# Two gate rows of a two-block kernel: 32-column ones matmuls and row copies in place of full-width sums

## The chip, the cores and the metric

One core of one Trainium2 chip runs the whole kernel. The time is device microseconds of one execution, the median of several; a profiled execution gives the trace, whose span runs from the first to the last instruction.

## What is computed

Two transformer blocks follow each other over 256 tokens of width 1024, all in float32. The first is modulated by a vector `c`: six rows of 1024 come from one matrix product, and two of them, `gt1` and `gt2`, gate the two branches of the block.

```python
mod = jax.nn.silu(c) @ w_ada[l] + b_ada[l]
sh1, sc1, gt1, sh2, sc2, gt2 = jnp.split(mod[:, None, :], 6, axis=-1)
...
o = jnp.concatenate([o_mla, o_ret.astype(o_mla.dtype)], axis=-1) @ w_out[l]
x_new = x + gt1 * o
x_new = x_new + gt2 * conv_ffn(modulate(rmsnorm(x_new, g_norm2[l]), sh2, sc2),
                               w_up[l], conv_w[l], conv_b[l], w_down[l])
```

The change touches `gt1` and `gt2` alone. The mixer of the block (latent attention, `w_uq` and `w_ukv` among its weights, and retention) and the second block stay as they are.

## The kernel before

The 256 tokens lie on partitions in two tiles of 128. Each float32 product is made of three matmuls of a high and a low part: a weight tile of 128x1024 (512 KB) is loaded by a DMA from SyncE's queue into one of five `raw` buffers (L211, L213), ScalarE casts it to the high part (L223, or L230 with a gain), VectorE takes the difference for the low part (L226, L231), and TensorE uses both (L186). A `raw` buffer comes free when the low part is made, and SyncE's next load waits for that. SyncE issues in program order, so a transfer that waits holds all that stand behind it.

The instructions of each engine are put in order by a scheduler that goes by estimated costs and priorities; a change in one place can move instructions around it.

The modulation rows come in two ways. Rows 0 and 1 are made on TensorE at the start (`ada_unit`). Rows 2 to 5 are made by `tick` (L518 to L534), which is called between other pieces of work: it loads one of eight `w_ada` tiles of a row (L524), and VectorE multiplies it by `silc`, one value for each partition, and adds it to an accumulator `g` of 128x1024 (L527, L530). After the eighth tile `ada_done` (L497) sums the accumulator over its 128 partitions with a matmul against a tile of ones. For rows 3 and 4 (shift and scale of the second branch) this is done in four matmuls of 32 columns of ones (L509), each of which puts 256 of the 1024 sums onto 32 partitions of one PSUM tile `tr`. For rows 2 and 5, the gates, two matmuls with 128 columns of ones (L503) put 512 sums each on all 128 partitions, and VectorE adds them (L505) onto `gt1` or `gt2`, tiles `bc` of 128x1024 that hold the bias row on every partition. Two DMAs (L494, L495, issued by L127 in `bc_row`) spread the bias from DRAM at about 64 us.

```python
                for i in range(2):
                    t = tr_tile()
                    ac = slice(i * 512, (i + 1) * 512)
                    nc.tensor.matmul(t, lhsT=ones, rhs=acc[:, ac], start=True, stop=True)
                    d = dst[:, i * 512:(i + 1) * 512]
                    nc.vector.tensor_tensor(out=d, in0=d, in1=t, op=ALU.add)
```

Around gate 1 (110 us) the program is in the input projection and the latent attention's `w_uq`. The `w_uq` product for the first 128 tokens goes into the two `at` tiles of PSUM, ScalarE reads them (L676), VectorE rotates 32 columns of each head (L631, L635, and the sum L637), and TensorE transposes the result (L682); then the same for the second 128 tokens in the same `at` tiles. The keys follow from `w_ukv` (L695). Two DMAs copy rotated keys inside SBUF, from 32 partitions to 32 others, four times each (L658). Around gate 2 (232 us) it is in the retention's heads (L772 to L807), and the `w_out` tiles arrive. `gt1` is read by VectorE behind `w_out`'s matmuls (L920) and `gt2` behind `w_down`'s (L1320).

Of the kernel before, what the change touches and what calls it, by code (L numbers as in the profile page):

```python
# [9 lines left out]
F32 = mybir.dt.float32  # L10
# [4 lines left out]
ALU = mybir.AluOpType  # L15
# [3 lines left out]
P = 128  # L19
# [39 lines left out]
ROW_COLS = {}  # L59
_o = 0  # L60
for _n, _w in (("g_ret", 512), ("onorm", 128), ("sinks", 8), ("ret_decay", 8), ("g_final", 1024),
               ("g_mix_post", 1024), ("g_x_post", 1024), ("g_ffn_post", 1024), ("g_mix_pre", 1024), ("b_gt1", 1024), ("b_gt2", 1024)):
    ROW_COLS[_n] = (_o, _o + _w)
    _o += _w
NROW = _o
# [17 lines left out]
def body(tc, A, out):  # L83
    nc = tc.nc
    es = ExitStack()
    with es:
        _body(nc, tc, A, out, es)


def _body(nc, tc, A, out, es):  # L90
# [18 lines left out]
    def tr_tile():  # L109
        return ps.tile([P, 512], F32, tag="tr", name="tr", bufs=2)  # L110
# [12 lines left out]
    def bc_row(dst, name, a=0, b=None):  # L123
        o, e = ROW_COLS[name]
        e = e if b is None else o + b
        o = o + a
        nc.sync.dma_start(dst, A["rows"][0:1, o:e].broadcast_to([P, e - o]))  # L127
# [3 lines left out]
    ones = cp.tile([P, P], F32, name="ones")  # L131
# [157 lines left out]
    with ExitStack() as e1:  # L289
        p1 = lambda name, bufs=1: e1.enter_context(tc.tile_pool(name=name, bufs=bufs))  # L290
        s8 = p1("s8p")
        s = p1("s1")
# [4 lines left out]
        c1 = s.tile([P, NC1 - 128], F32, name="c1")  # L297
# [40 lines left out]
        def ada_fm(acc, bias, dst, ns=1):  # L338
            rows = ada_rows(acc)
            t = tr_tile()  # L340
            for b in range(2):
                nc.tensor.transpose(t[:, b * P:(b + 1) * P], rows[:, b * P:(b + 1) * P], ident)
            tv = t[:, 0:256].rearrange("p (b q n) -> p n q b", b=2, q=4)
            for i in range(ns):
                nc.vector.tensor_tensor(out=dst[:, 8 * i:8 * i + 8].rearrange("p (q b) -> p q b", b=2), in0=tv[:, i, :, :],
                                        in1=FM(bias).rearrange("p (q b) -> p q b", b=2), op=ALU.add)

        def scale_gain(dst, sc, gname):
            nc.vector.scalar_tensor_tensor(out=dst, in0=sc, scalar=1.0, in1=FM(gname), op0=ALU.add, op1=ALU.mult)
# [141 lines left out]

        gt1 = bct()
        gt2 = bct()
        bc_row(gt1, "b_gt1")  # L494
        bc_row(gt2, "b_gt2")  # L495

        def ada_done(g, acc):  # L497
            if g in (2, 5):
                dst = gt1 if g == 2 else gt2
                for i in range(2):  # L500
                    t = tr_tile()
                    ac = slice(i * 512, (i + 1) * 512)
                    nc.tensor.matmul(t, lhsT=ones, rhs=acc[:, ac], start=True, stop=True)  # L503
                    d = dst[:, i * 512:(i + 1) * 512]
                    nc.vector.tensor_tensor(out=d, in0=d, in1=t, op=ALU.add)  # L505
            else:
                t = tr_tile()
                for q in range(4):
                    nc.tensor.matmul(t[32 * q:32 * q + 32, 0:256], lhsT=ones[:, 0:32],  # L509
                                     rhs=acc[:, q * 256:(q + 1) * 256], start=True, stop=True)  # L510
                ada_fm(t, "b_sh2" if g == 3 else "b_sc2", B2 if g == 3 else A2)
            if g == 4:
                scale_gain(A2, A2, "g_norm2")
# [357 lines left out]
    c2 = s2.tile([P, NCST2], F32, name="c2")  # L871
# [532 lines left out]
    for g in range(1, 6):  # L1404
        nb = 4 if g < 5 else 2
        sg = G4()
        for part, mk, us in ((0, tr_tile, ones_w2["gate"][g]), (1, at_tile, ones_w2["up"][g])):
# [3 lines left out]
            for i in range(nb // 2):  # L1411
                c = slice(i * 512, (i + 1) * 512)
                if part == 0:
                    nc.vector.tensor_tensor(out=sg[:, c].rearrange("p (j n) -> p j n", j=2),
                                            in0=accs[i].rearrange("p (j n) -> p j n", j=2),
                                            in1=rbc.unsqueeze(1).broadcast_to([P, 2, T]), op=ALU.mult)
# [17 lines left out]
def _constants():  # L1434
    f = np.float32
    pos = np.arange(T)

    def ang(p, dim):
        inv = (f(10000.0) ** (-np.arange(0, dim, 2, dtype=f) / f(dim))).astype(f)
        return (p.astype(f)[:, None] * inv[None, :]).astype(f)  # L1440

    ar, ac = ang(pos // 64, 16), ang(pos % 64, 16)
    mcos = np.concatenate([np.cos(ar), np.cos(ar), np.cos(ac), np.cos(ac)], 1)
    msin = np.concatenate([-np.sin(ar), np.sin(ar), -np.sin(ac), np.sin(ac)], 1)
    aq = ang(pos, 128)
    rcos, rsin = np.cos(aq), np.concatenate([-np.sin(aq), np.sin(aq)], 1)
    halves = lambda a: np.concatenate([a[:P], a[P:]], 1)
    p = np.arange(P)[:, None]
    j = np.concatenate([np.arange(P)[:, None], P + np.arange(P)[:, None]], 1)
    dl = np.arange(384)[None, :] - 128 - p  # L1450
    i = np.broadcast_to(np.arange(T)[None, :], (P, T))
    c1 = [np.eye(P), halves(mcos), halves(msin), halves(rcos), halves(rsin),
          np.concatenate([255 - j, j], 1), dl + 0 * p, i + 1, T - i]
    c1 = np.concatenate([np.asarray(a, f) for a in c1], 1)
    assert c1.shape == (P, NCST1)
    q = np.arange(P)
    causal = (p // 64 == q[None, :] // 64) & (p <= q[None, :])
    ck = np.arange(T)[None, :] // 64
    cq = 2 + p // 64
    ok = (ck <= cq) & (ck >= cq - 2)  # L1460
    c2 = [causal, np.where(ok, 0.0, -1e30)]
    c2 = np.concatenate([np.asarray(a, f) for a in c2], 1)
    assert c2.shape == (P, NCST2)
    return np.ascontiguousarray(c1), np.ascontiguousarray(c2)


def _layout(I):
    g = lambda n: np.asarray(I[n])
    fmv = lambda a: a.reshape(-1, P).T
    lb = g("hgrn_lb_2")  # L1470
    cw = g("conv_w")[0]
    fm = {"c": g("c"), "c_ctx": g("c_ctx"), "g_norm1": g("g_norm1"), "g_norm2": g("g_norm2"), "g_q": g("g_q"),
          "g_kv": g("g_kv"), "conv0": cw[0], "conv1": cw[1], "conv2": cw[2], "conv_b": g("conv_b"),
          "g_mem": g("g_mem_2"), "g_mix_pre": g("g_mix_pre_2"), "g_x_pre": g("g_x_pre_2"),
          "g_ffn_pre": g("g_ffn_pre_2"), "lb0": lb[0], "lb1": lb[1], "b_sh1": g("b_ada")[0, 0:1024], "b_sc1": g("b_ada")[0, 1024:2048],
          "b_sh2": g("b_ada")[0, 3072:4096], "b_sc2": g("b_ada")[0, 4096:5120]}
    order = np.array([0, 4, 1, 5, 2, 6, 3, 7])
    rows = {"g_ret": g("g_ret"), "onorm": g("hgrn_onorm_2"), "sinks": g("sinks_2"),
            "ret_decay": g("ret_decay"), "g_final": g("g_final"), "g_mix_post": g("g_mix_post_2"),
            "g_x_post": g("g_x_post_2"), "g_ffn_post": g("g_ffn_post_2"), "g_mix_pre": g("g_mix_pre_2"), "b_gt1": g("b_ada")[0, 2048:3072],  # L1480
            "b_gt2": g("b_ada")[0, 5120:6144]}
    w_in2 = g("w_in_2")[0]
    qa = w_in2[:, :512].reshape(D, 8, 64)[:, order].reshape(D, 512)
    w_in2 = np.concatenate([qa, w_in2[:, 512:]], 1)
    w_out2 = g("w_out_2")[0]
    w_out2 = np.concatenate([w_out2[:512].reshape(8, 64, D)[order].reshape(512, D), w_out2[512:]], 0)
    ukv = g("w_ukv")[0].reshape(256, 8, 2, 64).transpose(0, 2, 1, 3).reshape(256, 1024)
    c1, c2 = _constants()
    arrays = {
        "fm": np.concatenate([fmv(fm[n]) for n in FM_COLS], 1),  # L1490
        "rows": np.concatenate([rows[n].reshape(1, -1) for n in ROW_COLS], 1),
        "cst1": c1, "cst2": c2,
        "x": g("x")[0], "ctx": g("ctx")[0], "mem": g("mem_2")[0], "w_ada": g("w_ada")[0], "w_in": g("w_in")[0],
        "w_uq": g("w_uq")[0], "w_ukv": ukv, "w_out": g("w_out")[0], "w_up": g("w_up")[0], "w_down": g("w_down")[0],
        "w_in_2": w_in2, "w_out_2": w_out2, "wq_x": g("wq_x_2")[0], "wk_x": g("wk_x_2")[0], "wv_x": g("wv_x_2")[0],
        "wo_x": g("wo_x_2")[0], "w_gate": g("w_gate_2")[0], "w_up2": g("w_up_2")[0], "w_down2": g("w_down_2")[0],
    }
    return {n: np.ascontiguousarray(a) for n, a in arrays.items()}
# [17 lines left out]
```

## Time and profile before

| | before |
|---|---|
| median of 3 runs | 853.47 us (852.82 to 855.85) |
| profiled execution | 853.53 us |
| its span | 851.7 us |
| TensorE busy | 820.4 us, 96% of the span |
| VectorE busy | 575.3 us, 68% |
| ScalarE busy | 463.2 us, 54% |
| GpSimd busy | 52.7 us, 6% |
| DMA | 154.22 MB, mean 181 GB/s |
| mean granted clock | 0.994 of full speed |

The shares are means over the whole span, and say little on one place. A row of a timeline gives the start, the time in us, the engine and line, the operation and its operands, and in brackets how long the engine had stood idle and for what. SPq is SyncE's queue, where DMAs are issued; the time there is that of the issue, and a DMA's landing is told apart, in the DMA view. PE is TensorE, DVE is VectorE, ACT is ScalarE.

### The profile page before, as it was taken

The numbers are of one execution on the slowest core, as the hardware profiler recorded it, in microseconds if no ns is written. First come the engines' busy times: TensorE is split into PE (matmuls) and PEld (weight loads), VectorE is DVE, ScalarE is ACT, GpSimd is POOL, SyncE is SP. The second block draws the span as 40 slices with busy tenths as digits, with TensorE's granted clock in tenths as the row PEclk, the third lists the DMA queues.
The fourth block names the chain that finished last, engine by engine and source line by source line (L and its number), as shares of the span: only waits on it lengthen the run. The fifth ranks groups of instructions, "written<-read, shape, count | busy, mean of one in ns | idle before, by whom it ended". The sixth has DMA issues, their size and how long they took to land.

```text
span 851.7 us, 12981 instructions
## 1 busy us (share of the span) xinstructions
PE 820.4 (96%) x4978; PEld 691.3 (81%) x4978; DVE 575.3 (68%) x881; ACT 463.2 (54%) x749; POOL 52.7 (6%) x91
## 2 busy tenths in 40 slices
PE   6999988999999999999999999999999999999996
PEld 5767966766687899999997877777788899999995
DVE  4339767996697797667577766775847865656642
ACT  6739262324565675555454757664636844545531
POOL 1100020110110000000002200001001100000000
PEclk9999998999999999999999999999999999999999
DMA  8998786874154566666664553443623676666511
GB/s 289 312 311 274 239 260 206 291 232 134 50 161 141 177 227 197 183 189 182 191 188 149 163 147 121 124 145 114 194 92 120 185 226 191 181 189 188 183 50 50
DMA packets 65150, 154.22 MB, mean 181 GB/s; under 512 B 5184, under 2 KB 10816, under 8 KB 65088
## 3 DMA queue, kind: packets, MB, share of 16 engines
q1 hardware_dynamic: 65088, 153.39, 57.6%
q8 instruction: 39, 0.64, 0.3%
q14 instruction: 23, 0.19, 0.1%
HBM read 151.80 MB, written 1.05 MB: 179 GB/s over the span
## 4 chain that ended last, share of the span: by engine, by line
PE 66%; ACT 3%; DVE 3%; issue 1%; POOL 1%; DVEq 0%; POOLq 0%; ACTq 0%
PE acc L186 32%; PE at L256 12%; PE tr L256 12%; PE tr L168 1%; PE at L1280 1%; PE at L1258 1%; PE tr L1199 1%; DVE xl L226 1%; ACT junk L144 1%; ACT xh L223 1%; PE at L1149 1%; PE at L1151 1%; PE tr L743 0%; PE at L772 0%; PE at L789 0%
## 5 line engine op out<-in xcount | busy, mean ns | idle before, releaser
L223 ACT CAST wh<-raw 128x1024 fp32r<-128x1024 f32 (+1 forms) x90 | 91.0, 1013 | 101.5 <-PE acc L186 27.4
L226 DVE TENSOR_TENSOR wl<-raw,wh 128x1024 fp32r<-128x1024 f32 (+1 forms) x87 | 102.3, 1178 | 46.7 <-ACT wh L223 45.7
L226 DVE TENSOR_TENSOR xl<-raw,xh 128x1024 fp32r<-128x1024 f32 x68 | 84.6, 1248 | 43.0 <-ACT xh L223 42.7
L223 ACT CAST xh<-raw 128x1024 fp32r<-128x1024 f32 x68 | 70.9, 1047 | 55.0 <-PE tr L256 24.6
L186 PE MATMUL acc<-wh,xTh 128*128 128x512 f32 (+2 forms) x272 | 100.0, 394 | 0.3 <-ACT xTh L160 0.3
L186 PE MATMUL acc<-wh,xTl 128*128 128x512 f32 (+2 forms) x272 | 97.3, 382 | 0.0
L186 PE MATMUL acc<-wl,xTh 128*128 128x512 f32 (+2 forms) x272 | 96.7, 380 | 0.5 <-DVE wl L226 0.5
L231 DVE SCALAR_TENSOR_TENSOR wl<-raw,fm,wh 128x512 fp32r<-128x512 f32 (+3 forms) x96 | 67.2, 743 | 42.9 <-ACT wh L230 42.4
L230 ACT ACTIVATE wh<-raw,fm 128x512 fp32r<-128x512 f32 (+3 forms) x96 | 63.7, 712 | 36.5 <-issue 16.5
L186 PEld LDWEIGHTS acc<-wh,xTh 128*128 128x128 f32 x272 | 50.3, 189 | 12.0 <-issue 2.4
L186 PEld LDWEIGHTS acc<-wl,xTh 128*128 128x128 f32 x272 | 50.3, 188 | 11.3 <-issue 2.3
L186 PEld LDWEIGHTS acc<-wh,xTl 128*128 128x128 f32 x272 | 50.4, 188 | 9.6 <-issue 1.0
L186 PE MATMUL acc<-xh,xTl 128*128 128x512 f32 x144 | 53.5, 397 | 0.0
L186 PE MATMUL acc<-xl,xTh 128*128 128x512 f32 x144 | 53.3, 396 | 0.1
L186 PE MATMUL acc<-xh,xTh 128*128 128x512 f32 x144 | 53.2, 397 | 0.0
L231 DVE SCALAR_TENSOR_TENSOR xl<-raw,fm,xh 128x512 fp32r<-128x512 f32 (+1 forms) x44 | 33.3, 797 | 17.8 <-ACT xh L230 17.7
L186 PE MATMUL acc<-xh,g 128*128 128x512 f32 x160 | 44.5, 391 | 0.0
L230 ACT ACTIVATE xh<-raw,fm 128x512 fp32r<-128x512 f32 (+1 forms) x44 | 31.2, 756 | 22.5 <-issue 13.0
L530 DVE SCALAR_TENSOR_TENSOR g<-raw,silc,g 128x1024 f32<-128x1024 f32 x28 | 35.8, 1279 | 6.7 <-DMA raw<-in_w_ada_dram 6.7
L186 PE MATMUL acc<-wh,g 128*128 128x512 f32 x128 | 36.4, 391 | 0.0
L186 PEld LDWEIGHTS acc<-xh,g 128*128 128x128 f32 x160 | 29.7, 188 | 5.8
L186 PEld LDWEIGHTS acc<-xl,xTh 128*128 128x128 f32 x144 | 26.8, 188 | 6.3 <-DVE xl L226 1.1
(375 smaller groups left out, 1751.0 us busy)
## 6 DMA issues: line engine op xcount, KB each, us to landing
raw<-in_w_up_dram SPq DMA_DIRECT2D x66, 512.0 KB, 3.9
raw<-in_w_ada_dram SPq DMA_DIRECT2D x48, 512.0 KB, 5.3
raw<-in_w_down_dram SPq DMA_DIRECT2D x44, 512.0 KB, 3.5
raw<-in_w_in_dram SPq DMA_DIRECT2D x38, 512.0 KB, 3.9
raw<-in_w_gate_dram SPq DMA_DIRECT2D x22, 512.0 KB, 4.0
raw<-in_w_out_dram SPq DMA_DIRECT2D x16, 512.0 KB, 3.6
raw<-in_wk_x_dram SPq DMA_DIRECT2D x8, 512.0 KB, 6.3
raw<-in_wv_x_dram SPq DMA_DIRECT2D x8, 512.0 KB, 5.7
```

The lines of the kernel that those rows point to most:

```text
L144: nc.scalar.activation(junk[:, 0:a.shape[-1]], a, AF.Square, scale=n ** -0.5, accum_out=ss)
L168: nc.tensor.transpose(t[:, j * P:(j + 1) * P], src[:, (b + j) * P:(b + j + 1) * P], ident)
L186: nc.tensor.matmul(accs[i], lhsT=xl if f == 2 else xh, rhs=wl[i] if f == 1 else wh[i], start=first and f == 0, stop=last and f == 2)
L223: nc.scalar.copy(wh[:, 0:n], raw[:, 0:n])
L226: eng.tensor_tensor(out=wl[:, 0:n], in0=raw[:, 0:n], in1=wh[:, 0:n].bitcast(F32), op=ALU.subtract)
L230: nc.scalar.activation(wh[:, s], raw[:, s], AF.Copy, scale=gains[k])
L231: nc.vector.scalar_tensor_tensor(out=wl[:, s], in0=raw[:, s], scalar=gains[k], in1=wh[:, s].bitcast(F32), op0=ALU.mult, op1=ALU.subtract)
L256: nc.tensor.matmul(accs[b // 2][:, (b % 2) * T:(b % 2 + 1) * T], lhsT=wt[:, o:o + P], rhs=xt[:, k, :], start=k == 0 and fl == 0 and b % 2 ...
L530: nc.vector.scalar_tensor_tensor(out=ada_cur[g], in0=raw, scalar=silc[:, k, 0:1], in1=ada_cur[g], op0=ALU.mult, op1=ALU.add)
L1149: nc.tensor.matmul(o[cs, hs], lhsT=ATs[cs, cols], rhs=ih[cs, hs], start=True, stop=cg == 0)
L1151: nc.tensor.matmul(o[cs, hs], lhsT=qi[:, cols], rhs=Sst[cg - 1][:, hs], start=False, stop=True)
L1199: nc.tensor.matmul(sc[:, j * nk:(j + 1) * nk], lhsT=qTs[pr_, hd * P:(hd + 1) * P], rhs=kTs[pr_, 0:nk], start=True, stop=True)
```

## The change

All four rows that `tick` makes are now summed by the four 32-column matmuls. For the gates, VectorE adds the bias to the `tr` tile in one instruction of 128x256 and writes the sum into a tile `bgt`, of which partitions 0, 32, 64 and 96 matter: partition 32q holds quarter q of the row. Then four DMAs from SyncE's queue (L507 in the new numbering) each read one of these partitions, 256 values, and write them to all 128 partitions of a quarter of `gt1` or `gt2`: 1 KB to each of 128 partitions, 128 KB in all. The bias comes with one load of 128x512 (256 KB) from a new array, zero but in those four partitions; the two spread loads of 512 KB each are gone.

```diff
-        bc_row(gt1, "b_gt1")
-        bc_row(gt2, "b_gt2")
+        bgt = s.tile([P, 512], F32, name="bgt")
+        nc.sync.dma_start(bgt, A["bgt"])

         def ada_done(g, acc):
+            t = tr_tile()
+            for q in range(4):
+                nc.tensor.matmul(t[32 * q:32 * q + 32, 0:256], lhsT=ones[:, 0:32],
+                                 rhs=acc[:, q * 256:(q + 1) * 256], start=True, stop=True)
             if g in (2, 5):
                 dst = gt1 if g == 2 else gt2
-                for i in range(2):
-                    t = tr_tile()
-                    ac = slice(i * 512, (i + 1) * 512)
-                    nc.tensor.matmul(t, lhsT=ones, rhs=acc[:, ac], start=True, stop=True)
-                    d = dst[:, i * 512:(i + 1) * 512]
-                    nc.vector.tensor_tensor(out=d, in0=d, in1=t, op=ALU.add)
+                rows = bgt[:, 0:256] if g == 2 else bgt[:, 256:512]
+                nc.vector.tensor_tensor(out=rows, in0=t[:, 0:256], in1=rows, op=ALU.add)
+                for q in range(4):
+                    nc.sync.dma_start(dst[:, q * 256:(q + 1) * 256],
+                                      rows[32 * q:32 * q + 1, :].unsqueeze(1).broadcast_to([1, P, 256]))
             else:
-                t = tr_tile()
-                for q in range(4):
-                    nc.tensor.matmul(t[32 * q:32 * q + 32, 0:256], lhsT=ones[:, 0:32],
-                                     rhs=acc[:, q * 256:(q + 1) * 256], start=True, stop=True)
                 ada_fm(t, "b_sh2" if g == 3 else "b_sc2", B2 if g == 3 else A2)
```

The lines below the change count one less than before. The order of instructions differs between about 70 and 285 us, and is the same after that.

SyncE's queue at gate 1, about 106 to 115 us of the run before (`raw` is a weight buffer, `bc` is `gt1`):

```order
 L213 DMA raw<-in_w_in_dram 128x2x512
-L524 DMA raw<-in_w_ada_dram 128x1024 x3
+L523 DMA raw<-in_w_ada_dram 128x1024 x2
+L507 DMA bc<-bgt 128x1x256 x4
+L523 DMA raw<-in_w_ada_dram 128x1024
 L211 DMA raw<-in_w_ukv_dram 128x1024 x2
+L657 DMA s_1271<-s_1269 32x4x512
```

The four copies stand ahead of one `w_ada` tile and both `w_ukv` tiles, and they wait for VectorE's add.

ScalarE at the same place, where L230 is the cast of the two `w_ukv` tiles and L676 (now L675) the read of the `at` tiles of the first 128 tokens:

```order
+L653 COPY s_1269<-tr 32x512
 L230 ACTIVATE wh<-raw,fm 128x1024
-L160 CAST g_1171<-tr 128x2x128 x2
-L676 ACTIVATE g_1342<-at,rq_1176 128x384
-L654 COPY s_1265<-tr 32x512
-L676 ACTIVATE g_1342<-at,rq_1176 128x384
+L675 ACTIVATE g_1346<-at,rq_1180 128x384 x2
 L230 ACTIVATE wh<-raw,fm 128x1024
```

Both reads stand behind the first cast, before and now; nothing that could go ahead of them is left between.

VectorE some microseconds later, where L530 (now L529) is the accumulate of a `w_ada` tile and L637 (now L636) the sum that ends the rotation of the first 128 tokens:

```order
 L231 SCALAR_TENSOR_TENSOR wl<-raw,fm,wh 128x1024
-L631 TENSOR_TENSOR s1k<-g_1342,c_92 128x256
-L635 TENSOR_TENSOR s1k<-g_1342,c_92 128x16x8 x2
-L530 SCALAR_TENSOR_TENSOR g_1334<-raw,silc,g_1334 128x1024
-L637 TENSOR_TENSOR g_1342<-s1k 128x8x32
+L630 TENSOR_TENSOR s1k<-g_1346,c_92 128x256
+L634 TENSOR_TENSOR s1k<-g_1346,c_92 128x16x8 x2
+L636 TENSOR_TENSOR g_1346<-s1k 128x8x32
 L231 SCALAR_TENSOR_TENSOR wl<-raw,fm,wh 128x1024
```

The accumulate no longer stands ahead of the sum.

SyncE's queue at gate 2, about 230 us of the run before (`bc` is `gt2`):

```order
 L213 DMA raw<-in_w_in_dram 128x2x512 x3
-L211 DMA raw<-in_w_out_dram 128x1024 x8
+L211 DMA raw<-in_w_out_dram 128x1024 x6
+L507 DMA bc<-bgt 128x1x256 x4
+L211 DMA raw<-in_w_out_dram 128x1024 x2
 L213 DMA raw<-in_w_up_dram 128x2x512 x4
```

The four copies stand ahead of the last two `w_out` tiles and of `w_up`.

## Rows read from the trace of the kernel before

**Rows 1.** Busy time by stretch: us of PE, PEld, DVE, ACT, POOL; clock, DMA share, GB/s.

```profile
60.00:70.00 10.00, 8.91 (x48) 5.67 (x48) 6.53 (x17) 7.65 (x13) 0.00 (x0) 1.00 0.85 289
...
126.00:130.00 4.00, 0.00 (x0) 0.00 (x0) 1.67 (x3) 0.95 (x2) 0.00 (x0) 0.87 1.05 187
130.00:134.00 4.00, 3.99 (x14) 3.45 (x15) 3.36 (x6) 1.17 (x2) 0.00 (x0) 0.50 1.01 331
134.00:138.00 4.00, 4.00 (x20) 3.30 (x19) 1.93 (x3) 1.07 (x2) 0.00 (x0) 0.78 0.81 315
...
150.00:160.00 10.00, 10.00 (x56) 7.46 (x55) 9.78 (x17) 3.37 (x7) 0.00 (x0) 1.00 0.88 296
```

**Rows 2.** Chain of waits, gate 2: start us, us, what.

```profile
231.24 1.05 PE tr L503 x2
...
233.19 0.86 PE tr L503 x2
```

**Rows 3.** Timeline of all engines, gate 1, 108 to 115 us.

```profile
110.06 1.88 PE L503 MATMUL tr<-g,ones 128*128 128x512 f32 x4
...
111.36 0.68 DVE L505 TENSOR_TENSOR bc<-bc,tr 128x512 f32<-128x512 f32 x1
111.47 2.53 SPq L211 DMA_DIRECT2D raw<-in_w_ukv_dram  x2
...
113.69 0.50 PE L186 MATMUL acc<-wl,xTh 128*128 128x512 f32 x1 [0.53 <-DVE wl L226]
```

**Rows 4.** DMA view, 110 to 115 us: GB/s in 40 slices, packets, issues with us to landing.

```profile
GB/s 410 344 410 344 311 426 344 262 328 328 328 360 262 360 393 393 328 262 328 328 328 328 328 393 360 393 393 328 492 393 328 426 459 360 360 361 459 328 524 262
DMA packets 510, 1.81 MB, mean 361 GB/s; under 512 B 55, under 2 KB 55, under 8 KB 510
...
raw<-in_w_ukv_dram SPq DMA_DIRECT2D x2, 512.0 KB, 4.8
```

**Rows 5.** PE's waits, 60 to 80 us: total us, times, longest us.

```profile
PE acc L186 <- DVE wl L231: 1.4, 3, 0.5
```

**Rows 6.** Timeline of PE, the 32-column sums of row 3.

```profile
163.26 0.64 PE L509 MATMUL tr<-g,ones 128*32 128x256 f32 x8
```

**Rows 7.** The copies inside SBUF, line 658: issue ns and landing us, min/median/max.

```profile
L658 SPq DMA_DIRECT2D s<-s x2: 755/1080/1405, 122.3 to 123.1; - x2
...
DMA to landing us min/median/max: 8.4/8.7/8.9
```

**Rows 8.** DMA view, 125 to 130 us, while those copies run.

```profile
DMA packets 371, 0.90 MB, mean 180 GB/s; under 512 B 44, under 2 KB 44, under 8 KB 370
...
q1 hardware_dynamic: 370, 0.89, 103.5%
```

**Rows 9.** Timeline of ACT, 118 to 131 us.

```profile
118.32 1.16 ACT L230 ACTIVATE wh<-raw,fm 128x1024 fp32r<-128x1024 f32 x1
...
125.90 1.04 ACT L676 ACTIVATE g<-at,rq 128x384 f32<-128x384 f32 x2
```

**Rows 10.** Timeline of PE, 120 to 137 us: the second w_uq product and what follows.

```profile
123.71 0.51 PE L186 MATMUL at<-wh,s 128*128 128x384 f32 x2
...
130.01 1.94 PE L682 MATMUL tr<-ident,g 128*96 128x128 f32 x8 [4.05 <-DVE g L637]
131.60 1.20 PE L695 MATMUL at<-g,wh 128*128 128x512 f32 x2
```

**Rows 11.** Timeline of DVE, 116 to 132 us: the accumulate ahead of the rotation's sum.

```profile
128.33 1.28 DVE L530 SCALAR_TENSOR_TENSOR g<-raw,silc,g 128x1024 f32<-128x1024 f32 x1 [4.52 <-DMA raw<-in_w_ada_dram]
```

**Rows 12.** Timeline of DVE, gate 2.

```profile
232.50 0.68 DVE L505 TENSOR_TENSOR bc<-bc,tr 128x512 f32<-128x512 f32 x1
```

**Rows 13.** DMA view, 232 to 240 us: issues, KB each, us to landing.

```profile
raw<-in_w_out_dram SPq DMA_DIRECT2D x2, 512.0 KB, 3.6
```

**Rows 14.** Timeline of ACT, gate 2: the cast of the seventh w_out tile.

```profile
239.80 1.05 ACT L223 CAST xh<-raw 128x1024 fp32r<-128x1024 f32 x1 [0.73 <-DMA raw<-in_w_out_dram]
```

**Rows 15.** Timeline of PE, gate 2: a retention head's output matmuls.

```profile
243.08 0.71 PE L801 MATMUL acc<-s1k 128*128 128x128 f32 x4
```

More of the change, by code (lines that the diff above doesn't have):

```diff
@@ L61 @@
 for _n, _w in (("g_ret", 512), ("onorm", 128), ("sinks", 8), ("ret_decay", 8), ("g_final", 1024),
-               ("g_mix_post", 1024), ("g_x_post", 1024), ("g_ffn_post", 1024), ("g_mix_pre", 1024), ("b_gt1", 1024), ("b_gt2", 1024)):
+               ("g_mix_post", 1024), ("g_x_post", 1024), ("g_ffn_post", 1024), ("g_mix_pre", 1024)):
     ROW_COLS[_n] = (_o, _o + _w)
@@ L1479, in _layout @@
             "ret_decay": g("ret_decay"), "g_final": g("g_final"), "g_mix_post": g("g_mix_post_2"),
-            "g_x_post": g("g_x_post_2"), "g_ffn_post": g("g_ffn_post_2"), "g_mix_pre": g("g_mix_pre_2"), "b_gt1": g("b_ada")[0, 2048:3072],
-            "b_gt2": g("b_ada")[0, 5120:6144]}
+            "g_x_post": g("g_x_post_2"), "g_ffn_post": g("g_ffn_post_2"), "g_mix_pre": g("g_mix_pre_2")}
+    bgt = np.zeros((P, 512), np.float32)
+    bgt[::32, 0:256] = g("b_ada")[0, 2048:3072].reshape(4, 256)
+    bgt[::32, 256:512] = g("b_ada")[0, 5120:6144].reshape(4, 256)
     w_in2 = g("w_in_2")[0]
@@ L1491, in _layout @@
         "rows": np.concatenate([rows[n].reshape(1, -1) for n in ROW_COLS], 1),
-        "cst1": c1, "cst2": c2,
+        "cst1": c1, "cst2": c2, "bgt": bgt,
         "x": g("x")[0], "ctx": g("ctx")[0], "mem": g("mem_2")[0], "w_ada": g("w_ada")[0], "w_in": g("w_in")[0],
```

## The prediction

> **What bounds the kernel now.** I read the table of stretches first [rows 1]: TensorE is the engine that is nearly always busy (8.91 us of the ten from 60 us, all of the ten from 150 us), and the one hole near the change is the stretch 126 to 130 us, in which it does nothing. Then the chain of waits at the second gate [rows 2]: both gate matmuls stand on it, 1.05 and 0.86 us. Then the timeline of the first gate [rows 3], for what follows there, and the DMA view of the same time [rows 4]: 110 to 115 us moves 361 GB/s, all sixteen engines at work. So there the transfers are full too, and whatever is put into SyncE's queue there pushes back what stands behind it. 0.5% of this kernel, 4.3 us, is about what a measurement can tell from no change.
>
> **The change, part by part.** The profiled run took 853.53 us, 0.06 above the median of 853.47; I add to 853.53.
>
> *Loads.* Two bias rows of 512 KB each leave, a tile of 256 KB comes, all at 63.7 us. At 361 GB/s that is 768 KB, 2.1 us of transfers. TensorE's waits there are for VectorE's splits, 1.4 us in all between 60 and 80 us [rows 5], none for a load, and I take nothing; the bounds are 0 and -2.1 us.
>
> *Matmuls.* Gate 1: 1.88 us for two full-width matmuls become four 32-column ones, 0.64 us by the group that exists already for g = 3 [rows 6]. The 1.2 us saved is lost at once: at 113.69 us TensorE waits for VectorE's w_in split anyway, 0.53 us, and what starts that split is a load, not the gate. Gate 2: 1.05 + 0.86 = 1.91 us on the chain become 0.64: -1.27 us. VectorE's two adds of 0.68 us per gate [rows 3] become one of half that width, some 0.4 us; VectorE does not set the end at either place.
>
> *The eight copies.* Four per gate, each 128 KB out of one partition into 128. They go into SyncE's queue, each waiting on VectorE's add, ahead of w_ukv at gate 1 and ahead of the seventh w_out tile at gate 2 (the order above). No row shows a copy out of one partition. The nearest are the two s<-s copies at 122 us, 256 KB each out of 32 partitions: their issue takes SyncE 755 and 1405 ns, and they land after 8.4 and 8.9 us [rows 7]. While they run the sixteen engines stay full but move 180 GB/s [rows 8], where loads moved 361: one half. One reading is that a copy runs at the speed of the part of SBUF that it reads from: 32 partitions half of it, one partition a sixteenth. That gives 361/16 = 22.6 GB/s, 5.8 us for 128 KB. As 361 is a mean of loads from DRAM, I also take the best slice of that stretch, 524 GB/s [rows 4], of which a sixteenth is 32.8 GB/s, 4.0 us. From below the bound is a copy as fast as any load: 128 KB at 361 GB/s, 0.36 us. I take the slow reading, because the one copy inside SBUF that the trace has is so slow, and in it the middle of its two rates, 27.7 GB/s: 4.73 us a copy, 18.9 us a gate.
>
> Here the Trainium skill speaks against the change (page "SBUF — State Buffer", section "Door 1: The DMA port swizzle"): four neighbouring partitions lie behind one of sixteen ports, measured at 27.6 GB/s, and partitions 32 apart share a port. By its 27.6 GB/s a copy would be an estimated 4.75 us, and the total 0.2 us above mine; by the row's 22.6 GB/s it would be 8.6 us above. That 180 is half of 361 agrees with its table, in which 32 partitions reach half the ports; that one partition has a sixteenth no row shows.
>
> *Gate 1 on the path.* w_ukv is issued at 111.47 us and lands 4.8 us later [rows 3, 4], at 116.3. With the four copies ahead it lands 18.9 us later, 135.2. ScalarE now has w_ukv's cast ahead of the two reads (L675) that free the `at` tiles, so TensorE's second half of w_uq waits for it: the cast takes 1.16 us, the two reads 1.04 us [rows 9], and TensorE goes on at 137.4 us. Before, its hole ended at 130.01 us, 4.05 us long [rows 10], since the rope sum stood behind an accumulate that waited 4.52 us for its w_ada tile [rows 11]; in the new order that accumulate is behind the rope sum. After the hole the granted clock is 0.50 (the 1.2 GHz level), 0.87 before it and 0.78 after [rows 1]: it fell about 3 us after TensorE had stopped and was at half from about 129.0 to 135.8 us, 5.75 us of it with TensorE at work. I put the same 5.75 us behind the new, longer hole. The work between the hole and the keys' matmuls is now twelve w_uq matmuls, 2.25 us (123.71 to 125.96), and eight transposes, 1.59 us at half clock (130.01 to 131.60), so 0.8 at full: together 3.05 us at full, which at that clock takes 5.93 us: the keys' first matmul, L694 (L695 before), at 143.3. Before, it began at 131.60 with 4.16 us of half clock ahead, worth a start at 133.7 at full clock. Gate 1 costs +9.6 us.
>
> *Gate 2 on the path.* The add ends at about 232.9 us (it began at 232.50) [rows 12]. The transfers are idle there, so the copies start at once and hold the sixteen engines for 18.9 us; the seventh w_out tile, 3.6 us from issue to landing [rows 13], lands at 255.4. Before, its cast began at 239.80, having waited for that landing [rows 14]. That is +15.6 us. ScalarE's cast stands ahead of the copy (L774) and the exponentials (L777) that the next head's output matmuls read, so TensorE stops before those, which began at 243.08 us [rows 15]. A stop this long lowers the clock as the one at 126 us did: from the three stretches 126 to 138 us, 5.75 us at half, +2.9 us. With -1.27 us from the matmuls gate 2 costs +17.2 us.
>
> *No one else waits.* The gates are read behind w_out's and w_down's matmuls (L920, L1320), later than any landing above. If that cover went, it would be the landing itself that is paid.
>
> Sum: 853.53 + 9.6 + 17.2 = 880.3, so 880 us. With 4.0 or 5.8 us a copy the eight give 874.5 or 889.
>
> **The rivals.**
>
> *Copies like s<-s.* The four copies of a gate are 512 KB as those two are, and take 8.7 us together, whatever they read from. For it: it is the row itself, no extrapolation. Against: those 8.7 us hold a wait behind loads already queued. Gate 1: 111.8 + 8.7 + 4.8 = 125.3 for w_ukv, TensorE at 127.5, L694 at 133.4: -0.3 us. Gate 2: 232.9 + 8.7 + 3.6 = 245.2, +5.4 + 2.9 - 1.27 = +7.0. 860 us, 855 to 866.
>
> *Cheap copies, and faster.* If a copy costs no more than its bytes at 361 GB/s, only SyncE's issue is left, four times the median 1.08 us of the s<-s issues, 4.3 us. At gate 1 w_ukv lands at 121.2 us and the reads end at 123.4, before TensorE has done its other work (125.96 less the 2.25 us of w_uq). The hole and the half clock are gone, since the accumulate is out of the way: L694 at 126.8, up to -6.9 us. VectorE, busy 9.78 of the ten us from 150 [rows 1], can't give all of it; I take two thirds, -4.6. Gate 2: +1.0 - 1.27 = -0.3. 848.7 us, 846 to 853. It decides as soon as four copies take less than about 6 us. For it: 361 GB/s out of sixteen engines. Against: no copy inside SBUF in this trace ran near that.
>
> *Nothing but noise.* The order of the program differs from 70 to 285 us for reasons besides the copies, and the stretch could close up around them: within 2 us of before.
>
> **How the numbers follow.** Slow single-partition copies 0.45, copies like s<-s 0.22, cheap ones 0.26, nothing 0.07. Faster than 849.2 us comes from two thirds of the cheap case, 0.17. Within 0.5%: the rest of it 0.09, the nothing 0.07, and 0.02 of the s<-s case: 0.18. Slower: 0.65. The range of 849 to 889 us leaves out 0.16 of the cheap case and 0.04 above the upper price. As cases of both signs hold chances, the likeliest one's own range is 874 to 889.
>
> **What the profile would show.** Right: the copies land 19 us and more after the first one's issue, with transfers full at a rate far under 180 GB/s; TensorE idle some 14 us near 123 to 137 us, ended by ScalarE or VectorE behind the landing of w_ukv, and some 12 us near 243 us behind w_out; clock at 0.5 after each. Wrong: copies landing within 9 us of issue, or TensorE full in both places, or SyncE's own issue times as the longest wait.

## The result, and the profile after

The changed kernel takes 881.88 us (median of 6 runs, 879.02 to 884.28), the kernel before 852.14 (6 runs, 850.66 to 855.85): a ratio of 1.033, 95% interval 1.031 to 1.035, 3.3% slower. The forecast was 880.

The first lines of the page of the changed kernel, the span and the busy time of each engine:

```profile
span 879.5 us, 13009 instructions
...
PE 823.1 (94%) x4986; PEld 692.1 (79%) x4986; DVE 574.8 (65%) x879; ACT 463.4 (53%) x749; POOL 54.1 (6%) x91
```

No engine has much more to do: TensorE is busy 823.1 us against 820.4, VectorE 574.8 against 575.3. The span is 27.8 us longer, so the time went into waits. TensorE's waits between 100 and 300 us in the changed kernel, with the total, the number and the longest, begin with the first two of these lines; the third is a smaller one to which I come back:

```profile
PE at L771 <- ACT s1k L774: 14.4, 1, 14.4
PE at L186 <- ACT g L675: 13.5, 1, 13.5
...
PE tr L168 <- DVE bgt L505: 1.1, 1, 1.1
```

The two are one wait each, and the 4.05 us behind L637 [rows 10] is gone. SyncE's timeline at gate 1, then at gate 2, and the line of the copies (nanoseconds of issue, then us to landing, each minimum, median, maximum):

```profile
113.52 8.84 SPq L507 DMA_DIRECT2D bc<-bgt  x4
122.46 3.59 SPq L523 DMA_DIRECT2D raw<-in_w_ada_dram  x1
126.15 5.10 SPq L211 DMA_DIRECT2D raw<-in_w_ukv_dram  x2
...
244.90 8.28 SPq L507 DMA_DIRECT2D bc<-bgt  x4
253.29 9.06 SPq L211 DMA_DIRECT2D raw<-in_w_out_dram  x2
```

```profile
L507 SPq DMA_DIRECT2D bc<-bgt x8: 557/1406/5190, 113.5 to 248.4; - x8
...
DMA to landing us min/median/max: 7.0/12.7/15.8
```

The copies land after up to 15.8 us, and SyncE itself is held: the four issues of a gate take 8.84 and 8.28 us, one of them 5.19. The DMA view of the changed kernel from 113 to 131 us, GB/s in 40 slices of 0.45 us and the share of the sixteen engines' time:

```profile
GB/s 382 364 209 105 57 34 27 27 20 36 25 27 21 36 25 23 25 36 25 23 25 34 48 84 73 36 23 32 32 23 20 41 73 146 100 41 64 75 93 164
...
q1 hardware_dynamic: 754, 1.22, 78.9%
```

To compare with [rows 4] and [rows 8]: the engines are at work 78.9% of the time and move 20 to 36 GB/s for most of the 12 us from 115 us on. What TensorE waited for at gate 1 and how it went on, ScalarE's timeline and then TensorE's:

```profile
138.07 1.15 ACT L230 ACTIVATE wh<-raw,fm 128x1024 fp32r<-128x1024 f32 x1 [15.20 <-DMA raw<-in_w_ukv_dram]
139.12 1.03 ACT L675 ACTIVATE g<-at,rq 128x384 f32<-128x384 f32 x2
```

```profile
139.74 1.16 PE L186 MATMUL at<-wh,s 128*128 128x384 f32 x2 [13.53 <-ACT g L675]
...
144.82 0.73 PE L694 MATMUL at<-g,wh 128*128 128x512 f32 x2
```

And at gate 2, ScalarE and then TensorE:

```profile
265.55 1.04 ACT L223 CAST xh<-raw 128x1024 fp32r<-128x1024 f32 x1 [16.38 <-DMA raw<-in_w_out_dram]
```

```profile
268.27 2.08 PE L771 MATMUL at<-g,g 128*128 128x128 f32 x8 [14.44 <-ACT s1k L774]
```

Busy time by stretch, columns as in [rows 1]; the clock is the first number behind POOL:

```profile
116.00:120.00 4.00, 3.69 (x13) 2.58 (x12) 2.10 (x10) 2.55 (x9) 2.84 (x7) 0.58 0.82 27
...
128.00:132.00 4.00, 0.00 (x0) 0.00 (x0) 0.00 (x0) 0.00 (x0) 0.00 (x0) 0.70 0.74 131
132.00:136.00 4.00, 0.00 (x0) 0.00 (x0) 1.28 (x1) 0.00 (x0) 0.00 (x0) 0.50 0.95 274
136.00:140.00 4.00, 0.26 (x1) 0.26 (x1) 0.75 (x1) 1.93 (x3) 0.00 (x0) 0.50 1.04 188
140.00:144.00 4.00, 4.00 (x18) 3.61 (x19) 2.97 (x6) 2.23 (x4) 0.00 (x0) 0.60 1.04 299
...
262.00:266.00 4.00, 0.00 (x0) 0.00 (x0) 0.00 (x0) 0.45 (x1) 0.00 (x0) 0.50 0.87 267
266.00:270.00 4.00, 1.73 (x8) 1.73 (x9) 3.15 (x6) 3.53 (x7) 0.00 (x0) 0.50 0.46 151
270.00:274.00 4.00, 4.00 (x23) 3.79 (x22) 1.71 (x4) 2.50 (x5) 0.00 (x0) 0.63 0.61 190
```

**Where the 28 us came from**, by the same instructions in both traces. VectorE's add of gate 1 starts 1.7 us later (113.07 against 111.36). From it to the keys' matmuls at full clock, 31.75 us against 22.34 (111.36 to the 133.7 of the prediction): +9.4. From there to the add of gate 2, 99.6 against 98.8: +0.8. From that add, 244.46 against 232.50, to the first read of `gt1`, 291.87 against 263.87: 47.4 against 31.4, +16.0. Together 28.0, and nothing is given back after that.

### The profile page after: what moved, and what is told of

Read it like the earlier page. It is cut to its first block, busy times and chain, and to the rows that moved or that the text cites. A ratio compares the mean times of both kernels' runs of the same rounds, so it can differ in the third digit from the quotient of the medians.

```text
span 879.5 us, 13009 instructions
## 1 busy us (share of the span) xinstructions
PE 823.1 (94%) x4986; PEld 692.1 (79%) x4986; DVE 574.8 (65%) x879; ACT 463.4 (53%) x749; POOL 54.1 (6%) x91
## 4 chain that ended last, share of the span: by engine, by line
PE 63%; ACT 4%; DVE 3%; DMA 1%; issue 1%; SPq 1%; POOL 1%; DVEq 0%; POOLq 0%; ACTq 0%
PE acc L186 30%; PE at L256 12%; PE tr L256 12%; DMA raw<-in_w_out_dram 1%; PE tr L168 1%; ACT xh L223 1%; SPq L507 1%; PE at L1279 1%; PE at L1257 1%; PE tr L1198 1%; DVE xl L226 1%; ACT junk L144 1%; PE at L1148 1%; PE at L1150 0%; PE tr L742 0%
## 5 line engine op out<-in xcount | busy, mean ns | idle before, releaser
L186 PE MATMUL acc<-wl,xTh 128*128 128x512 f32 (+2 forms) x272 | 99.4, 390 | 0.8 <-DVE wl L226 0.8
L231 DVE SCALAR_TENSOR_TENSOR wl<-raw,fm,wh 128x512 fp32r<-128x512 f32 (+3 forms) x96 | 67.2, 742 | 46.9 <-ACT wh L230 46.3
L230 ACT ACTIVATE wh<-raw,fm 128x512 fp32r<-128x512 f32 (+3 forms) x96 | 63.7, 712 | 51.0 <-issue 16.5
L186 PEld LDWEIGHTS acc<-wh,xTh 128*128 128x128 f32 x272 | 50.4, 189 | 13.5 <-issue 2.3
L529 DVE SCALAR_TENSOR_TENSOR g<-raw,silc,g 128x1024 f32<-128x1024 f32 x28 | 37.8, 1349 | 14.1 <-DMA raw<-in_w_ada_dram 13.9
L231 DVE SCALAR_TENSOR_TENSOR xl<-raw,fm,xh 128x512 fp32r<-128x512 f32 (+1 forms) x44 | 33.3, 797 | 17.8 <-ACT xh L230 17.7
L230 ACT ACTIVATE xh<-raw,fm 128x512 fp32r<-128x512 f32 (+1 forms) x44 | 31.1, 756 | 22.5 <-issue 13.0
```

Of the source, the lines that this page charges most:

```text
L186: nc.tensor.matmul(accs[i], lhsT=xl if f == 2 else xh, rhs=wl[i] if f == 1 else wh[i], start=first and f == 0, stop=last and f == 2)
L230: nc.scalar.activation(wh[:, s], raw[:, s], AF.Copy, scale=gains[k])
L231: nc.vector.scalar_tensor_tensor(out=wl[:, s], in0=raw[:, s], scalar=gains[k], in1=wh[:, s].bitcast(F32), op0=ALU.mult, op1=ALU.subtract)
L529: nc.vector.scalar_tensor_tensor(out=ada_cur[g], in0=raw, scalar=silc[:, k, 0:1], in1=ada_cur[g], op0=ALU.mult, op1=ALU.add)
```

## The experiments

All runs are on one core, beside runs of the kernel before (851.5 to 852.0 us in the median). A run without an interval was executed once; single runs of the kernel before lie up to 6 us from its median, so those are read by their traces.

**What is read, or that it is a copy.** My theory: the price is that of reading one partition. Rivals: a copy inside SBUF is slow by itself, or costs what the s<-s copies did.

```diff
-                                      rows[32 * q:32 * q + 1, :].unsqueeze(1).broadcast_to([1, P, 256]))
+                    nc.sync.dma_start(dst[:, q * 256:(q + 1) * 256], rows)
```

> The four copies of a gate read all 128 partitions of bgt (256 values of each partition go to the same partition of the gate tile) in place of one; bytes, number of copies, their place in SyncE's queue and the order of all engines stay. The gate tiles then hold other values than the sums. If the price comes from reading one partition (my theory): the copies land within 5 us of their issue in place of 7.0 to 15.8, the stretch in which the engines move under 30 GB/s is gone, TensorE's waits of 13.5 and 14.4 us shrink under 2 us, and the time is 846 to 856 us. If a copy inside SBUF is slow whatever it reads from (rival 1): landing and waits as in the changed kernel, 875 to 885 us. If it costs as the s<-s copies did (rival 2): about 8.7 us for four, 857 to 866 us.

849.87 us. The line of the copies in this run:

```profile
L507 SPq DMA_DIRECT2D bc<-bgt x8: 536/598/608, 113.7 to 231.5; - x8
...
DMA to landing us min/median/max: 2.0/2.1/2.1
```

Same bytes, same place in the queue, landed after a sixth of the time (median 2.1 against 12.7 us), and SyncE is not held. No wait of TensorE from 100 to 300 us is over 1.5 us in total. That is the theory's case. It also gives an idea of the time of the change without its price, but no gain is shown: one run of 849.87 us lies within the spread of the kernel before (848.72 to 857.52 beside it).

**Reading 32 partitions**, four times each, which keeps the repeated reading.

```diff
-                    nc.sync.dma_start(dst[:, q * 256:(q + 1) * 256],
-                                      rows[32 * q:32 * q + 1, :].unsqueeze(1).broadcast_to([1, P, 256]))
+                    nc.sync.dma_start(dst[32 * q:32 * q + 32, :].rearrange("p (j n) -> p j n", j=4),
+                                      rows[32 * q:32 * q + 32, :].unsqueeze(1).broadcast_to([32, 4, 256]))
```

> Each of the four copies of a gate reads 32 partitions (0 to 31, 32 to 63, ...) and writes 32 partitions, four times 1 KB to each: again 128 KB and 128 pieces of 1 KB, in the same place of SyncE's queue. The gate tiles then hold other values. If the rate follows the number of partitions read (8 of 16 shares where one partition has 1): about 200 GB/s, 0.7 us for a copy, landing within 4 us, 847 to 856 us. If reading one place again and again (a broadcast source) is what is slow: copies land after more than 6 us, 858 us or more.

The line of the copies in this run:

```profile
L507 SPq DMA_DIRECT2D bc<-bgt x8: 593/605/745, 115.4 to 240.9; - x8
...
DMA to landing us min/median/max: 2.4/2.7/3.3
```

The copies landed after 2.4 to 3.3 us, the rate between 188 and 249 GB/s while those of gate 1 ran: the theory's number, and against repeated reading as the cause. The time was 859.35 us, which is where slow copies would have put it, though the copies were not slow. SyncE's timeline tells a part of the reason:

```profile
118.19 0.53 SPq L523 DMA_DIRECT2D raw<-in_w_ada_dram  x1
124.85 1.27 SPq L657 DMA_DIRECT2D s<-s  x2
126.17 1.96 SPq L211 DMA_DIRECT2D raw<-in_w_ukv_dram  x2
```

With these shapes the scheduler put the s<-s copies ahead of w_ukv, and they wait for ScalarE until 124.85 us, so w_ukv, free to go at 118.7, is issued 7.5 us late. TensorE waits 1.8 and 1.1 us behind it, and 2.1 us for VectorE's rotation ahead of that. Some 2.5 us had gone before the first gate (`bgt` is loaded at 66.2 us, the bias rows of the kernel before at 63.66). The run is a clean test of the copies and none of the total.

**Another place that is read.** The quarters go out to a DRAM row and come back in one spread load.

```diff
-                    nc.sync.dma_start(dst[:, q * 256:(q + 1) * 256],
-                                      rows[32 * q:32 * q + 1, :].unsqueeze(1).broadcast_to([1, P, 256]))
+                nc.gpsimd.dma_start(gd[k], rows.rearrange("(q i) n -> q i n", i=32)[:, 0, :])
+                nc.gpsimd.dma_start(dst, gd[k].rearrange("q n -> (q n)").unsqueeze(0).broadcast_to([P, 1024]))
```

> Each gate's four quarters go to a DRAM row (4 KB) and come back as one spread load of 512 KB from DRAM onto 128 partitions, both issued from GpSimd's queue. The same 512 KB reach the same 128 partitions as by the four copies; only the place that is read differs. If the price is that of reading one partition of SBUF: no stretch under 30 GB/s, waits under 3 us, 848 to 855 us. If spreading 512 KB from one small place is slow wherever it lies: waits over 5 us at both gates, 862 us or more.

850.18 us, ratio 0.998 (0.996 to 1.000). The spread load of 512 KB lands after 4.5 and 4.8 us, where the four copies of the same bytes held everything for some 17:

```profile
L509 POOL DMA_DIRECT2D bc<-gd x2: 564/682/800, 121.6 to 235.0; - x2
...
DMA to landing us min/median/max: 4.5/4.7/4.8
```

So reading one small place again and again was slow here in SBUF, and not in DRAM.

**Which partitions share a way out.** In the changed kernel there is one short stretch at 84 and 73 GB/s among the 25s, at about 123 us, where the second copy ends and the third begins.

```diff
-                for q in range(4):
+                for q in (0, 2, 1, 3):
                     nc.sync.dma_start(dst[:, q * 256:(q + 1) * 256],
```

> The changed kernel with the four copies of a gate in the order of partitions 0, 64, 32, 96 in place of 0, 32, 64, 96; nothing else moves. In the changed kernel the engines move 27 GB/s during the copies but for one stretch of about a microsecond with 60 to 100 GB/s, where the second copy (partition 32) gives way to the third (partition 64). If partitions 32 apart are read through the same place and those 64 apart through another: such a stretch now comes at each of the three changes, some 2 us are saved at each of the two new ones, and the time is 870 to 876 us. If the stretch has to do with something else: no change, 878 to 884 us.

870.31 us, some 11 us less than the changed kernel from a change of order alone; TensorE's two long waits are 5.7 and 9.5 us in place of 13.5 and 14.4. The DMA view at gate 2, 18 us from where the copies begin, in slices of 0.45 us: first the changed kernel from 244 us, then this one from 238 us.

```profile
GB/s 0 0 0 0 14 34 27 34 32 16 27 34 30 16 27 36 30 16 27 36 27 18 27 36 41 100 36 34 20 32 23 34 20 32 50 50 50 66 93 93
```

```profile
GB/s 0 0 0 0 0 23 25 34 27 30 18 34 27 30 27 112 50 46 64 46 48 52 61 66 61 57 52 32 27 34 68 148 237 330 264 273 300 309 273 291
```

While partition 0 is read alone the rate is 27 as before; as soon as partition 64 is in the queue behind it, the two go together at 46 to 66 GB/s, for eleven slices, and the stretch that held the engines is over some 4 us sooner. Partitions 0 and 32, one behind the other, never do that. So it is not "one partition" but a place behind which several lie: 0 with 32, 64 with 96.

**Whose queue.** The copies from GpSimd's queue, SyncE's order as in the kernel before.

```diff
-                    nc.sync.dma_start(dst[:, q * 256:(q + 1) * 256],
+                    nc.gpsimd.dma_start(dst[:, q * 256:(q + 1) * 256],
```

> The eight copies are issued from GpSimd's queue in place of SyncE's; SyncE's queue then has the weight loads alone, in the order of the kernel before. If the loss comes only from the copies standing ahead of w_ukv and w_out in one queue: the loads go past them and the time is 848 to 854 us. If the sixteen engines are held by a copy whichever queue it comes from (my theory: each engine takes a piece of the slow copy between two pieces of a load): the loads land late all the same, by some half of the 17 us, 859 to 870 us. If nothing goes past: 876 us or more.

875.2 us, at the edge of "nothing goes past". w_ukv was issued at 113.55 us, right behind the add as in the kernel before (111.47 there, the add at 111.36), and landed 12.8 us later by the median of its two tiles. ScalarE's casts show that the two fared differently; the third line is the cast of the seventh w_out tile:

```profile
raw<-in_w_ukv_dram SPq DMA_DIRECT2D x2, 512.0 KB, 12.8
bc<-bgt POOLq DMA_DIRECT2D x4, 128.0 KB, 13.0
```

```profile
122.31 1.15 ACT L230 ACTIVATE wh<-raw,fm 128x1024 fp32r<-128x1024 f32 x1 [0.15 <-DMA raw<-in_w_ukv_dram]
...
133.34 1.15 ACT L230 ACTIVATE wh<-raw,fm 128x1024 fp32r<-128x1024 f32 x1 [7.98 <-DMA raw<-in_w_ukv_dram]
...
258.53 1.04 ACT L223 CAST xh<-raw 128x1024 fp32r<-128x1024 f32 x1 [15.79 <-DMA raw<-in_w_out_dram]
```

At gate 1 the first tile is cast 8.8 us after the issue, the second after 19.8, and TensorE waits 8.0 us in place of 13.5. At gate 2 the w_out tiles are issued at 240.81 us, 2.4 us behind the end of the add, and yet the seventh is cast only 20.1 us behind that end, against 20.7 in the changed kernel; TensorE waits 13.8 us in place of 14.4. My half holds for gate 1 and not for gate 2. The order in one queue is a part of the price at gate 1 and next to nothing at gate 2, where a copy holds the sixteen engines from whichever queue. At gate 1 the loads were issued 0.7 us ahead of the first copy (114.24), at gate 2 2.05 us behind it (238.76); that this makes the difference is not tested.

**One gate at a time.** Gate 1 or gate 2 keeps the old matmuls, adds and its spread bias row; the diff for gate 1, without the arrays of the bias (for gate 2 the same with g == 5, `gt2`):

```diff
+        bc_row(gt1, "b_gt1")
         def ada_done(g, acc):
+            if g == 2:
+                dst = gt1
+                for i in range(2):
...
+                return
             t = tr_tile()
```

> Gate 1 is made in the old way (two full-width matmuls onto a bias row spread from DRAM), gate 2 in the new way. If the two gates cost each for itself, gate 2 about 16 us: 868 us, with one wait of about 14 us in retention and gate 1's stretch as before the change. If the stretch at gate 1 was lost through the other edits (the order, the smaller bias load) and not through its copies: 877 us or more.

> Gate 2 in the old way, gate 1 in the new way. If the gates cost each for itself: gate 1 about 11 us, 863 us, with the wait of about 13 us before the second w_uq product and none in retention. If one gate's copies delay what the other's then find idle (not additive): the two runs' gains over the kernel before add to clearly more or less than 28 us.

871.44 and 865.83 us. Each has just its own long wait, 14.4 us in retention and 12.4 us before the second w_uq product. Over 852 the two are 19 and 14, together more than 28; but before the gates begin, the load of `bgt` at the start was issued at 67.3 and 65.5 us, against 63.9 in the changed kernel. From that load to the end of the span it is 802.4 and 798.6 us, and 788.0 in the kernel before from its first bias load (63.66): +14.4 and +10.6, together 25 of the changed kernel's 27.6. The gates cost each for itself, as far as single runs tell; the 2.6 us left over are within what those differ by.

**Ways to keep the shorter matmuls.** With the bias in all 32 rows of a quarter, all 128 partitions of `bgt` hold sums, and an engine can spread them.

```diff
-                    nc.sync.dma_start(dst[:, q * 256:(q + 1) * 256],
-                                      rows[32 * q:32 * q + 1, :].unsqueeze(1).broadcast_to([1, P, 256]))
+                    for r in range(4):
+                        nc.gpsimd.tensor_copy(dst[32 * r:32 * r + 32, q * 256:(q + 1) * 256],
+                                              rows[32 * q:32 * q + 32, :])
```

> The bias stands in all 32 rows of each quarter, so all 128 partitions of bgt hold sums, and GpSimd spreads each gate with sixteen copies of 32x256 in place of the DMAs; same result. If the loss lies in the copies' hold on the sixteen engines: both waits are gone and the time is 846 to 853 us, with some 1 to 3 us gained on the kernel before by the shorter matmuls. If GpSimd's copies slow VectorE, or the rest of the loss is in the order of the program: 853 to 860 us.

854.75 us, ratio 1.003 (1.001 to 1.005). A new wait took the place of the old. GpSimd's timeline, and then TensorE's first wait:

```profile
116.03 7.82 POOL L508 COPY bc<-bgt 32x256 f32<-32x256 f32 x16
123.94 0.79 POOL L139 TENSOR_SCALAR rs<-ss 128x1 f32<-128x1 f32 x3
```

```profile
PE tr L168 <- ACT s1k L644: 5.8, 1, 5.8
```

The sixteen copies of gate 1 stand ahead of the key norms' small steps, which ScalarE and then TensorE wait for. Two tries to move them behind. First by priority (`with tc.high_priority(offset=-600)` around gate 1's copies):

> As the run in which GpSimd spreads the gates, but the sixteen copies of gate 1 have a lower priority in the program's order, so that GpSimd takes the four norms' small steps (L139, L140) between them and not after all sixteen. There TensorE waited 5.8 us for a cast behind those steps, with GpSimd 7.8 us in the copies. If that wait is the loss: it falls under 1.5 us, and the time is 847 to 851 us, faster than before by 0.1 to 0.5%. If the gap has another cause, or GpSimd's copies slow VectorE: 852 to 855 us as there.

854.93 us, ratio 1.004 (1.003 to 1.006): a miss. The scheduler put the norms' steps between the copies, each step came behind one to four of them, and TensorE waited three times for the same casts, 2.3 us, and 1.6 us for a weight cast. Then by data: gate 1's copies add a column of zeros made from the last norm.

```diff
+        z = small(1, "z", 1)
+        nc.gpsimd.tensor_scalar(out=z, in0=r, scalar1=0.0, scalar2=None, op0=ALU.mult)
+        spread.pop()(z)
...
+                                nc.gpsimd.tensor_scalar(out=o, in0=i, scalar1=z[32 * q:32 * q + 32, 0:1],
+                                                        scalar2=None, op0=ALU.add)
```

> GpSimd spreads the gates by sixteen copies of 32x256 each, and those of gate 1 add a zero that is made from the last of the four norms, so that GpSimd cannot take them ahead of the norms' steps. No DMA copies, none of the waits of 5.8 us (copies ahead of the norms) or 2.3 us (copies between them). If these waits were what ate the gain of the shorter matmuls: TensorE has no wait over 1.5 us from 100 to 300 us, and the time is 846 to 850 us, faster than before by some 2 to 5 us. If GpSimd's copies cost VectorE or the order eats it: 851 to 855 us.

849.75 us, ratio 0.9985 (0.9968 to 1.0003). TensorE's longest wait there is 0.9 us, though GpSimd needs long:

```profile
118.75 0.81 POOL L140 TENSOR_TENSOR rs<-rs,mhalf 128x1 f32<-128x1 f32 x1
119.65 0.24 POOL L662 TENSOR_SCALAR z<-rs 128x1 f32<-128x1 f32 x1
119.99 24.39 POOL L515 TENSOR_SCALAR bc<-bgt,z 32x256 f32<-32x256 f32 x16
```

24 us on an idle engine, for a row that is first read 140 us later, cost nothing that these runs show. Last, gate 2 alone with GpSimd's copies, gate 1 in the old way:

> Gate 1 in the old way, gate 2 in four 32-column matmuls and GpSimd's sixteen copies. If the matmuls are worth 1.27 us at gate 2 and the copies nothing: 850 to 852 us, within noise of before. If GpSimd's copies slow the retention around them: 853 us or more.

850.40 us, ratio 1.000 (0.998 to 1.002). As expected, and below what the runs can tell apart. So the shorter matmuls are worth at most some 3 us by the intervals of the last two and of the DRAM row, and nothing above zero is shown. All three beat the changed kernel by over 3%; that one of them beats the kernel before is not shown.

## Why the prediction was right

- **What bounds.** Right. TensorE's work did not shrink or grow; the loads that the copies pushed back set the end.
- **Matmuls, adds, bias loads.** Gate 1's saving was lost at once, as said: TensorE waits 0.53 us for the same split at 115.55 us. "VectorE does not set the end at either place" was wrong at gate 1. The four matmuls end near 112.1 us, VectorE has a w_uq split (L231) ahead of the add, which begins at 113.07, and TensorE's next transposes into `tr` wait 1.15 us for the add (0.24 before). After that TensorE ran at half clock (0.50 from 116 to 118 us, 0.67 from 118 to 120; 1.00 before). In the changed kernel this cost nothing, since TensorE stood for w_ukv soon after; the run that reads 128 partitions has the same wait and the same fall of the clock (0.67 and 0.50), and no long wait to cover it. For gate 2's -1.27 us there is only the bound above. The 2.1 us of bias loads should read 2.2 (768 KB at 361 GB/s); the sum took nothing for them.
- **The price of a copy.** I took 4.73 us from the middle of two rates worked out from loads. Measured, one partition is read at 16 to 36 GB/s, around 27 (first nine slices of the copies at gate 2), so 4.8 us. That the middle was so near is luck: the two rates were sixteenths of loads from DRAM, and the choice between 4.0 and 5.8 us had no row. Nor was the 180 GB/s of [rows 8] the copies' own rate: 0.90 MB moved in those 5 us, where the two copies are 0.52 MB in all, so loads ran among them. The reason given, that the rate follows the part of SBUF that is read, is shown by 128 partitions (2.1 us landing), 32 (2.4 to 3.3 us) and one (up to 15.8 us). By the rule of the Trainium skill's page "SBUF — State Buffer", section "Door 1: The DMA port swizzle", it is 27.6 GB/s, and partitions 0 and 32 lie behind one port, 64 and 96 behind another; the trace agrees with both, the second by the run with the other order.
- **Four of them.** 18.9 us a gate was too much: the second and third overlap for a moment, at up to 100 GB/s. The prediction's "partitions 32 apart share a port" holds for 0 and 32 and for 64 and 96, as the two orders show, and not for 32 and 64, which are 32 apart too. From the add of gate 2 (end 244.87) to w_out's landing (265.52) it was 20.7 us, where the prediction had 22.5.
- **Gate 1, +9.6 us.** Measured +9.4. From the end of the add to TensorE's return 26.3 us against 25.6 forecast (111.8 to 137.4); the half-clock time after it was shorter, 3.5 us (139.74 to 143.2, by the 0.60 of 140 to 144 us) against 5.75. The two misses nearly cancel, which is luck.
- **Gate 2, +17.2 us.** Measured +16.0: 1.8 less from the copies, and 4.7 us at half clock (268.27 to 273.0, by the 0.63 of 270 to 274 us) in place of 5.75, 0.5 less. That makes 14.9. The other 1.1 us lie in two places. TensorE stopped before the next head's L771 and not, as forecast, before its output matmuls, and stood 14.44 us where the cast came 13.8 us later: 0.65. And only the second pair of the old matmuls, 0.86 us, stood behind the first add, from which the +16.0 is counted; the other 0.41 of the 1.27 lies ahead of it. By TensorE's own rows the sum closes: 14.44 us stopped, 2.35 lost at half clock, less 0.86, is 15.9.
- **What was not in the sum.** 1.7 us ahead of gate 1, where TensorE now waits 0.35 and 0.24 us near 106 us and the add comes late. Both waits are behind one w_in tile. SyncE issued it at 97.95 us before and at 98.14 in the changed kernel, and it landed after 5.7 and 7.3 us. ScalarE's cast of it began at 103.76 and at 105.50 us. In the run with the other order of copies and the one with the added column, where SyncE's queue has the same order up to there, it landed after 5.8 and 5.6 us; in the nine other runs it was 6.7 to 7.2. So it is not the copies, and the program alone does not settle it; whether the change makes the late landing likelier stays open, with one trace of the kernel before.
- **SyncE's issue.** The prediction named it as the mark of a wrong forecast if it were the longest wait. It was held 8.8 and 8.3 us a gate, but behind the copies: with 128 partitions read the same four issues took 0.6 us each, and with SyncE free of the copies (the run from GpSimd's queue) the seventh w_out tile came 0.6 us sooner at gate 2.
- **The rivals.** Copies at the price of s<-s (860 us) fell with the landing times. Cheap copies (848.7 us) came true to 1.2 us in the one run that reads 128 partitions. The time landed where it did because one partition was the expensive case, not because copies are.

## What to carry to other kernels

A DMA's price is also set by which partitions it reads, and how many: by the rates measured here, 128 KB out of one are 4.8 us, out of 32, at some 200 GB/s, 0.65 us. What stands behind it in its queue waits, and most of what comes from another queue does too. Ask of every added transfer what is issued behind it and who needs that next; a row that is read 140 us later doesn't belong ahead of a weight that is read now. If a row must be spread, let many partitions hold it, or send it through DRAM, or give it to an idle engine, and check that nothing urgent stands behind it there either.

## What the runs showed that I had not expected

- The order of four copies (partitions 0, 64, 32, 96 in place of 0, 32, 64, 96) changed the whole kernel by some 11 us in the one run made: two that are read through different places run together, though they were issued one behind the other.
- SyncE's issue of a DMA can take 5.19 us when the transfers ahead of it are slow, where the same one took 0.6 us when 128 partitions were read.
- A stop of TensorE of 13.5 us did not cost more clock than one of 4.05 us: 3.5 and 4.7 us at half clock after the long ones, 5.75 after the short one. By the 0.50 of the stretches 132 to 140 and 258 to 266 us it had been at the 1.2 GHz level for most of each long stop.
- GpSimd takes 388, 509 and 1327 ns (minimum, median and maximum) for a copy of 32x256 at gate 2, and 917, 1162 and 2546 ns for the same with an added column at gate 1.
